# Ranking tiles laid out by chunks, with masks put together by transfers, in the sparse-attention layer of a hybrid encoder step on Trainium2

## The chip, the cores and the metric

The kernel runs on one core of one Trainium2 chip. The metric is the device time of one execution in microseconds. The engines are TensorE (PE; its weight loads are PEld), VectorE (DVE), ScalarE (ACT), GpSimd (POOL) and SyncE (SP), which here only issues DMAs. ACT and POOL issue some DMAs too.

## What is computed

One inference step of a two-layer encoder over 576 tokens: a prompt of 512 new tokens and a sample of 64 tokens that continues a stream with 512 cached ones. Layer 0 mixes by pooling, layer 1 by sparse attention; a squared-ReLU MLP follows each. The change lies in layer 1. There an indexer scores every key for every query and only the best keys take part in the attention:

```python
logits = jnp.einsum('bthd,bsd->bths', qi, kidx) * (IDX_DIM ** -0.5)         # 8 indexer heads of 64
score = jnp.einsum('bths,bth->bts', jax.nn.relu(logits), wi)                # wi: a weight per token and head
adm = (kpos[None, :] // CHUNK) <= qchunk[:, None]                           # chunks of 64 tokens
score = jnp.where(adm[None], score, NEG)
_, idx = lax.top_k(score, n_sel)                                            # n_sel = min(256, L // 4)
...
s = jnp.einsum('btgrd,btkgd->btgrk', qg, kg) * (HEAD_DIM ** -0.5)           # 16 heads of 64, 4 key heads
s = jnp.where(valid[:, :, None, None, :], s, NEG)
p = jax.nn.softmax(s, axis=-1)
o = jnp.einsum('btgrk,btkgd->btgrd', p, vg)
```

For the prompt L is 512, so 128 keys are kept of the chunks up to the query's own; a query in the first two chunks keeps all it may see. For the sample L is 576, and 144 keys are kept.

## The kernel before, in words

Activations lie feature-major (features on partitions, tokens along the row). A float32 product is made of split operands (`wh` and the rest `wl`, and the same for activations, `xs`): ACT casts `wh` (L189), DVE or POOL subtracts for `wl` (L190), and PE runs three matmuls. The weights stream from memory as `raw` tiles. Names in the trace and in the order are those of tiles.

The function `attention` projects its input with PE (`project`, tile `pj` on PSUM, 48 matmuls of 288 columns for each block of 128 features), in this order: indexer keys `ki` with the indexer weights, two blocks of indexer queries (rotated in `rope_qi`, brought to tile `qi`), keys `k`, four pairs of blocks of queries `q0` to `q3` (rotated, written to memory by DMA, read back by group as `q`), and values `V`. Then a loop over 40 units runs the attention, and at its end the output projection `wo`; blocks of it for the first tokens, `wa`, are put between units.

Tokens are taken in attention tiles i = 0 to 4: 128 prompt tokens each for i = 0 to 3, and the 64 sample tokens for i = 4. Each i has 4 groups of heads, each of two units. The units of i = 0 and 1 alternate, then come those of 2, 3 and 4. A unit's steps are: scores `sc` on PE (L1334, for the sample L1344), a softmax whose maximum DVE takes while it adds the mask (L1304, output `p` and `nm`), the exponential on ACT, the scaling of `p` on POOL (L1311, L1313), transposes `pt` on PE (L1360, L1365) and the product with the values, `o` on PE.

The mask of a tile is its ranking tile `work1` to `work4`: 128 rows by 256, 384 or 512 keys, and for the sample 64 rows by 576. `index_scores(i)` computes it head by head: two matmuls into `ix` (L1253, four for the sample, L1258), a ReLU on ACT (L1261, L1264), and a multiply-add by the token's weight on DVE (L1273, L1275). For the sample this is done on POOL (L1269, L1271). `top_k(i)` then takes rounds on DVE: MAX8 (L1286) finds the eight largest of a row, MATCH_REPLACE8 (L1287) strikes them out; 16 rounds strike 128 keys, 18 rounds 144. A last TENSOR_SCALAR (L1290) turns what was struck into 0 and the rest into a large negative number. Queries of the first two chunks of the prompt rank nothing (`mask0`).

Where the scores are written is set by `pace`, a generator that `project` steps once for each k-block: it writes one head's scores, then as many blocks later as PACE says the next. It covers all heads of the three prompt tiles but one; the rest, and the sample's eight, are written in the unit loop (`steps`). `top_k` is called ahead of the first scores of its tile's attention. The final order on each engine is made by a scheduler with a timeline simulation; an engine runs its row in that order, and SP issues its DMAs in its own.

```python
units = [Unit(i, g, s) for g in range(NKV) for i in range(2) for s in range(2)]
units += [Unit(i, g, s) for i in range(2, 5) for g in range(NKV) for s in range(2)]
```

Of the kernel before, what the change touches and what calls it, by code (L numbers as in the profile page):

```python
# [37 lines left out]
PACE = (1, 2, 2)  # L38
PACED = 3 * NIDX - 1
# [17 lines left out]
def pool_dsa_kernel(ctx: ExitStack, tc: tile.TileContext, a, o):  # L57
# [89 lines left out]
    def raw_tile(pool=raws, n=2 * 264):  # L147
        return pool.tile([P, n], F32, tag="raw", name=uid("raw"))
# [21 lines left out]
    jobs.extend(("w_v", a["w_v"][j], 4 * 264) for j in range(2))  # L170
# [6 lines left out]
    def unit(n=512):  # L177

        return [weights.tile([P, 528], F32R, tag=t, name=uid(t))[:, :n] for t in ("wh", "wl")]
# [13 lines left out]
    class Stream:  # L193
# [5 lines left out]
        def room(self, mlp):  # L199

            if "more" not in phase:
                return ("raws", raws, 2 * 264) if len(self.live["raws"]) < 2 else None
            if mlp and len(self.live["more"]) < RAWS[1]:
                return "more", phase["more"], 512
            return ("raws", raws, 2 * 264) if len(self.live["raws"]) < RAWS[0] else None

        def fill(self):
            while jobs:
# [12 lines left out]
                (nc.sync if mlp else act).dma_start(raw[-1], src[:, i * n // 2:(i + 1) * n // 2])  # L221
# [873 lines left out]
    def attention(parts):  # L1095
# [21 lines left out]
        wi = const([P, 5, 8], "wi", pool=cst)  # L1117
# [52 lines left out]
        def rope_qi(g, started=()):  # L1170

            _, st = rope(True, started)
            for part, queue in enumerate((act, nc.sync)):
                for h in range(4):
                    for j in range(2):
                        at = part * 64 + j * 32
                        queue.dma_start(f32(qi[at:at + 32, 4 * g + h]), f32(st[j][32 * h:32 * h + 32, part, P:]))
# [31 lines left out]
        turnable = tmp("wi")  # L1209
        for h, pt in enumerate(pki):  # L1210
            act.activation(halves(turnable[0:32])[:, h], pt[64:96, :HT], AF.Copy, scale=NIDX ** -0.5)
        turned_wi = psum1("wi")[:, :5 * 32].rearrange("p (i c) -> p i c", i=5)
        for i in range(5):
            n = P if i < 4 else TS
            pe.transpose(turned_wi[:n, i], turnable[0:32, i * P:i * P + n], ident[0:32, 0:32])
        for n, i in ((P, slice(0, 4)), (TS, slice(4, 5))):
            ri = r[:n, i].rearrange("p (i c) -> p i c", c=1)
            dve.tensor_tensor(wi[:n, i], turned_wi[:n, i, :NIDX], ri.to_broadcast([n, i.stop - i.start, NIDX]), ALU.mult)
        qi = const([P, NIDX, T - P], "qi", F32R, phase["queries"])
# [3 lines left out]
        project(pt, next_block(), xs)  # L1223
        t1, t2, ki = tmp("t1"), tmp("t2"), tmp("ki")
# [12 lines left out]

        rope_qi(1, [bank_halves(pt)])
        cki = split_cache(a["cache_ki"], "cki", kis)

        work = [None] + [const([P, (i + 1) * P if i < 4 else TP + TS], f"work{i}", pool=phase["under"] if i == 1 else cst) for i in range(1, 5)]

        def index_scores(i):
            np_ = P if i < 4 else TS
            wk = work[i]
            n = wk.shape[1]
            q = qi[:, :, (i - 1) * P:(i - 1) * P + np_]
            on_pool = i == 4
            for h in range(NIDX):
                if i < 4:  # L1250
                    pf = psum1("ix")
                    for part in range(2):
                        pe.matmul(pf[:, :n], q[:, h], kis[:, part, :n], start=part == 0, stop=part == 1)  # L1253
                else:
                    pf = psum("ix")
                    for part in range(2):
                        for c in range(2):
                            pe.matmul(pf[:TS, c, :HT], q[:, h], cki[:, part, c * HT:(c + 1) * HT], start=part == 0, stop=part == 1)  # L1258
                if i < 4:
                    rl = pf  # L1260
                    act.activation(rl[:, :n], pf[:, :n], AF.Relu, scale=0.125)  # L1261
                else:
                    rl = tmp("rl")
                    act.activation(halves(rl[:TS]), pf[:TS, :, :HT], AF.Relu, scale=0.125)  # L1264
                wcol = wi[:np_, i, h:h + 1]
                if on_pool:
                    dst = rl[:np_, :n] if h else wk[:np_]
                    with behind(turned):
                        pool.tensor_tensor(dst, rl[:np_, :n], wcol.to_broadcast([np_, n]), ALU.mult)  # L1269
                        if h:  # L1270
                            pool.tensor_tensor(wk[:np_], wk[:np_], dst, ALU.add)  # L1271
                elif h == 0:
                    dve.tensor_scalar(wk[:np_], rl[:np_, :n], wcol, None, ALU.mult)  # L1273
                else:
                    dve.scalar_tensor_tensor(wk[:np_], rl[:np_, :n], wcol, wk[:np_], ALU.mult, ALU.add)  # L1275
                yield
            if i < 4:
                dve.memset(wk[0:64, i * P + 64:(i + 1) * P], NEG)

        def top_k(i):  # L1280

            wk = work[i]
            np_ = P if i < 4 else TS
            for _ in range(16 if i < 4 else 18):
# [367 lines left out]
```

## Time and profile before

| | |
|---|---|
| median of 3 runs | 1074.8 us (1072.69 to 1076.98) |
| profiled execution | 1075.7 us, its span 1073.9 us, granted clock 0.996 |
| busy of the span | PE 98%, PEld 95%, DVE 85%, ACT 59%, POOL 25% |
| scoring begins on DVE | 458.32 us |
| first softmax of a unit | 535.32 us |
| output projection begins | 654.41 us |

Busy time is that in which an engine runs at least one instruction; two matmuls overlap in their ends, so the start-to-start distance is what one costs. A timeline line reads: start, duration, engine, line, operation, output tile and inputs, shape, count, and in brackets the idle time ahead and what ended it. The windows cut the span into stretches, with each engine's busy time in them. "Mean ns of one" in a group is a duration, and the last part of its line is idle time ahead of the group's instructions.

### The profile page before, as it was taken

To read this page: it belongs to the slowest core of one execution; us is meant where nothing else is said; L and a number is where in the kernel's file an instruction comes from. 1 tells how busy PE (TensorE), PEld (TensorE's weight loads), DVE (VectorE), ACT (ScalarE), POOL (GpSimd) and SP (SyncE) were. 2 spreads that over 40 slices of the span, in tenths; PEclk is the share of its full clock that TensorE was granted. 3 is DMA by queue.
4 is the path that set the end of the run, shared out by engine and by line. 5 is a ranking of instruction groups with operands and counts; after the bars stand their busy time and mean duration, and the time that the engine had idled before them with its cause. 6 is when DMAs were issued, how large, how long until landed. Compare 5 with 4: busy or idle time off the path is not lost.

```text
span 1073.9 us, 21666 instructions
## 1 busy us (share of the span) xinstructions
PE 1048.8 (98%) x7947; PEld 1024.1 (95%) x7947; DVE 908.6 (85%) x1842; ACT 630.4 (59%) x1254; POOL 269.0 (25%) x285
## 2 busy tenths in 40 slices
PE   9999999999999999999989999999999999999996
PEld 8999999999999999999989888999999999999995
DVE  7889989879978996889789974689889879979984
ACT  8556457547646764353388776556457447647742
POOL 3200111111111100358767983000111111111001
PEclk9999999999999999999999999999999999999999
DMA  8333676676676565376542444433776777676522
GB/s 250 91 104 93 166 160 166 166 169 166 148 176 169 138 182 170 111 200 168 167 131 79 134 141 140 137 101 88 177 165 150 176 167 168 148 179 162 123 59 88
DMA packets 95514, 157.68 MB, mean 147 GB/s; under 512 B 14785, under 2 KB 26352, under 8 KB 95408
## 3 DMA queue, kind: packets, MB, share of 16 engines
q1 hardware_dynamic: 67952, 108.88, 33.7%
q0 software_dynamic: 15840, 28.84, 17.4%
q10 hardware_dynamic: 11616, 18.58, 5.7%
q8 instruction: 62, 1.02, 0.4%
q14 instruction: 44, 0.36, 0.1%
HBM read 141.18 MB, written 10.89 MB: 142 GB/s over the span
## 4 chain that ended last, share of the span: by engine, by line
PE 88%; DVE 4%; DMA 3%; ACT 2%; issue 1%; POOL 1%; ACTq 0%; SPq 0%; DVEq 0%; POOLq 0%
PE b L518 32%; PE c L518 16%; PE up L316 9%; PE a L518 8%; PE pj L316 7%; PE wo L316 3%; PE wa L316 2%; PE sc L1334 2%; PE pt L1360 1%; PE pb L1062 1%; PE v L1521 1%; DMA raw<-in_w_in 1%; PE o L1392 1%; PE dn L316 1%; DVE wl L190 1%
## 5 line engine op out<-in xcount | busy, mean ns | idle before, releaser
L189 ACT CAST wh<-raw 128x512 fp32r<-128x512 f32 (+1 forms) x316 | 194.5, 619 | 210.0 <-PE b L518 64.4
L190 DVE TENSOR_TENSOR wl<-raw,wh 128x512 fp32r<-128x512 f32 x294 | 210.5, 718 | 40.9 <-ACT wh L189 34.2
L518 PE MATMUL b<-u,wh 128*128 128x288 f32 x992 | 204.1, 296 | 2.3 <-ACT a L555 1.9
L518 PEld LDWEIGHTS b<-u,wh 128*128 128x128 f32 x992 | 159.8, 188 | 4.5 <-ACT a L555 3.1
L189 ACT CAST wh<-sum 128x512 fp32r<-128x512 f32 x165 | 102.3, 620 | 96.1 <-PE b L518 42.3
L518 PE MATMUL b<-u,wl 128*128 128x288 f32 x496 | 146.1, 296 | 0.4 <-DVE wl L190 0.4
L190 DVE TENSOR_TENSOR wl<-sum,wh 128x512 fp32r<-128x512 f32 x165 | 112.3, 687 | 22.3 <-ACT wh L189 20.8
L249 POOL DMA_DIRECT2D sum<-in_w_down x31 | 27.1, 891 | 336.6 <-DVE sum L271 65.0
L518 PE MATMUL c<-u,wh 128*128 128x288 f32 x496 | 103.0, 297 | 0.0
L518 PEld LDWEIGHTS b<-u,wl 128*128 128x128 f32 x496 | 93.1, 188 | 0.6 <-DVE wl L190 0.6
L316 PE MATMUL up<-xs,wh 128*128 128x288 f32 x512 | 89.4, 296 | 0.2
L484 DVE TENSOR_TENSOR u<-v,u 128x576 fp32r<-128x576 f32 (+3 forms) x106 | 83.1, 787 | 2.1 <-ACT u L481 1.6
L518 PEld LDWEIGHTS c<-u,wh 128*128 128x128 f32 x496 | 79.8, 188 | 1.3 <-ACT wh L189 1.1
L518 PE MATMUL b<-xt,wh 128*128 128x288 f32 x384 | 77.5, 295 | 0.0
L518 PE MATMUL b<-xs,wh 128*128 128x288 f32 x384 | 77.1, 295 | 0.0
L316 PEld LDWEIGHTS up<-xs,wh 128*128 128x128 f32 x512 | 74.7, 188 | 1.0 <-DVE v L470 0.7
L481 ACT CAST u<-v 128x576 fp32r<-128x576 f32 (+3 forms) x106 | 73.7, 699 | 3.3 <-DVE v L505 2.3
L518 PE MATMUL c<-u,wl 128*128 128x288 f32 x248 | 73.2, 295 | 0.0
L249 POOL DMA_DIRECT2D sum<-in_w_up x24 | 20.7, 863 | 202.4 <-DVE wl L190 101.0
L316 PE MATMUL pj<-xs,wh 128*128 128x288 f32 x352 | 62.7, 295 | 0.0
L518 PEld LDWEIGHTS b<-xt,wh 128*128 128x128 f32 x384 | 61.7, 188 | 0.0
L518 PEld LDWEIGHTS b<-xs,wh 128*128 128x128 f32 x384 | 61.1, 188 | 0.0
(294 smaller groups left out, 2728.6 us busy)
## 6 DMA issues: line engine op xcount, KB each, us to landing
raw<-in_w_up SPq DMA_DIRECT2D x128, 256.0 KB, 3.1
raw<-in_w_down SPq DMA_DIRECT2D x128, 256.0 KB, 3.0
raw<-in_w_o ACTq DMA_DIRECT2D x32, 256.0 KB, 3.4
sum<-in_w_down SPq DMA_DIRECT2D x31, 256.0 KB, 2.9
sum<-in_w_down POOLq DMA_DIRECT2D x31, 256.0 KB, 4.9
raw<-in_w_down POOLq DMA_DIRECT2D x31, 256.0 KB, 5.0
raw<-in_w_in ACTq DMA_DIRECT2D x30, 256.0 KB, 3.1
sum<-in_w_up SPq DMA_DIRECT2D x24, 256.0 KB, 3.1
```

Of the source, the lines that this page charges most:

```text
L189: act.copy(h, src)
L190: how["sub"].tensor_tensor(l, src, f32(h), ALU.subtract)
L249: pool.dma_start(s1, odd[:, 512:], accum_op=ALU.add)
L316: pe.matmul(pt[h][:, :m] if isinstance(pt, tuple) else pt[:, h, :m], wt, xs[k][:, part, c:c + m], start=(k == 0 and i == 0), stop=(k == n ...
L481: return act.copy(u[:, f, 0], v[:, f])
L484: return dve.tensor_tensor(u[:, f, 1], v[:, f], f32(u[:, f, 0]), ALU.subtract)
L518: ins = pe.matmul(bank[:, :HT], wt, ut, start=first and j == 0 and i == 0, stop=j == 3 and i == 2, skip_group_check=True)
L1062: pe.matmul(pt[:, c0:c0 + rhs.shape[1]], lhs, rhs, start=n == 0, stop=n == len(steps) - 1)
L1334: pe.matmul(pt[:, hh, :nw], q[:, 2 * s + hh], ks[g][:, part, :nw], start=part == 0, stop=part == 1)
L1360: pe.transpose(pp[:, c:c + P], pr[:, hh, kt * P:(kt + 1) * P], ident)
L1392: pe.matmul(o[64 * hh:64 * hh + 64, s * P:(s + 1) * P], V[:, kt, vs], pT[:, c:c + P], start=kt == 0, stop=kt == i)
L1521: pe.matmul(pt[:n, :256], xs[k][:, part, i * P:i * P + n], wt[:, sl], start=(k == 0 and j == 0), stop=(k == KT - 1 and j == 2))
```

## The change

Ranking tiles are laid out by chunks. Instead of tokens 128 to 255, 256 to 383, 384 to 511 and the sample, they are now (first token, rows, keys): (128, 64, 192), (192, 128, 320), (320, 128, 448), (448, 128, 576). In a tile of two chunks the first chunk sees 64 keys less. The last tile holds the last chunk of the prompt in rows 0 to 63 and the sample in rows 64 to 127. Its index scores are made in two halves of 288 keys, each of four matmuls: the prompt's queries with zeros where the sample's would be against the prompt's keys, and zeros followed by the sample's queries against the cached ones, added up on PSUM. Its last two rounds run on the sample's rows alone.

The attention tiles stay as they were, so their masks `mask1` to `mask4` are put together: a ranking tile is written in place in the next attention tile's mask, and after its `top_k` two DMAs on SP bring the lower rows of one to the upper rows of the mask ahead (`masks[i][64:128]`), and move the upper rows of its own down (`masks[i + 1][0:64]`). What the shorter rows lack POOL fills with the negative number.

All index scores are written inside the projection, paced by (1, 2, 2, 1), and all are done ahead of V. Of the four `top_k`, two are called ahead of the first unit of i = 1, one ahead of i = 2, one ahead of i = 3. POOL ranks nothing any more. The indexer queries go to memory and come back (24 DMAs on SP for each half `g`, in place of 16 on SP and ACT from tile to tile). The indexer weights are scaled on DVE by the norm's row, not on ACT, and turned by four transposes. The value weights are loaded without the 8 columns of indexer weights, so weight tiles are 512 wide and not 528.

```diff
-PACE = (1, 2, 2)
-PACED = 3 * NIDX - 1
+PACE = (1, 2, 2, 1)
+RANKED = ((128, 64, 192), (192, P, 320), (320, P, 448), (448, P, 576))
...
+                if kind == "w_v":
+                    act.dma_start(raw[-1].rearrange("p (k c) -> p k c", k=2), src.rearrange("p (k c) -> p k c", k=4)[:, 2 * i:2 * i + 2, :256])
...
-            for part, queue in enumerate((act, nc.sync)):
-                for h in range(4):
-                    for j in range(2):
-                        at = part * 64 + j * 32
-                        queue.dma_start(f32(qi[at:at + 32, 4 * g + h]), f32(st[j][32 * h:32 * h + 32, part, P:]))
+            qd = dram.tile([2, 2, P, T - P], F32, tag=f"qi{g}", name=f"qi{g}")
+            for part in range(2):
+                for j in range(2):
+                    nc.sync.dma_start(qd[part, j], f32(st[j][:, part, P:]))
+                for j in range(2):
+                    at = part * 64 + j * 32
+                    src = qd[part, j].rearrange("(h p) t -> p h t", h=4)
+                    for to, of in ((slice(0, TP - P), slice(0, TP - P)), (slice(TP - TS, TP), slice(TP - P, T - P))):
+                        nc.sync.dma_start(f32(qi[at:at + 32, 4 * g:4 * g + 4, to]), src[:, :, of])
...
-            act.activation(halves(turnable[0:32])[:, h], pt[64:96, :HT], AF.Copy, scale=NIDX ** -0.5)
+            dve.scalar_tensor_tensor(halves(turnable[0:32])[:, h], pk[64:96, :HT], NIDX ** -0.5, halves(norm.rb[0:32])[:, h], ALU.mult, ALU.mult)
...
+                    if last:
+                        for part in range(2):
+                            for keys in (kis, cki):
+                                t0 = TP - P - TS if keys is kis else TP - P
+                                pe.matmul(pf[:, :m], qi[:, h, t0:t0 + P], keys[:, part, at:at + m],
+                                          start=part == 0 and keys is kis, stop=part == 1 and keys is cki)
...
-                if on_pool:
-                    dst = rl[:np_, :n] if h else wk[:np_]
-                    with behind(turned):
-                        pool.tensor_tensor(dst, rl[:np_, :n], wcol.to_broadcast([np_, n]), ALU.mult)
-                        if h:
-                            pool.tensor_tensor(wk[:np_], wk[:np_], dst, ALU.add)
...
-            for _ in range(16 if i < 4 else 18):
+            for n in range(18 if i == len(RANKED) - 1 else 16):
+                rows = slice(0 if n < 16 else 64, RANKED[i][1])
                 m8 = small(8, "m8")
...
+            dve.tensor_scalar(wk, wk, -2e38, NEG, ALU.is_gt, ALU.mult)
+            if i:
+                nc.sync.dma_start(masks[i][64:128], wk[0:64, :(i + 1) * P])
+                nc.sync.dma_start(masks[i + 1][0:64], masks[i + 1][64:128])
...
-                mask = work[i]
+                mask = masks[i]
...
+            due = {1: 2, 2: 1, 3: 1}
...
-                    if u + AHEAD >= 4:
-                        next(index, None)
-                    if v.i not in ranked:
-                        ranked.add(v.i)
-                        while done[0] < v.i * NIDX and next(index, 1) is None:
-                            pass
-                        top_k(v.i)
+                    for _ in range(due.pop(v.i, 0)):
+                        top_k(next(rank))
                     v.scores()
...
+        for _ in index:
+            pass
         wv = [next_block(), next_block()]
```

What this does to the order of instructions shows best on DVE, at the first softmax of attention tile i = 3 (the first ISA row that reads a 512-wide mask; in the rows here MAX, MATCH_REPLACE and TENSOR_SCALAR are ranking, ISA is a softmax). Before (`work_5889` is tile i = 3, `work_5890` the sample):

```order
L1304 ISA nm_7792 128x1
L1290 TENSOR_SCALAR work_5889<-work_5889 128x512
L1286 MAX m_1487_8366<-work_5890 64x8
L1438 TENSOR_TENSOR ot_7290<-o_7765,ot_7290 128x2x128
L1287 MATCH_REPLACE work_5890<-m_1487_8366,work_5890 64x576
L1286 MAX m_1488_8369<-work_5890 64x8
L1287 MATCH_REPLACE work_5890<-m_1488_8369,work_5890 64x576
L1304 ISA p_7904,nm_7910<-sc_7905,work_5889 128x512
L1304 ISA nm_7910 128x1
```

After (`mask_5885` is the last ranking tile, `mask_5884` the mask of i = 3):

```order
L1440 TENSOR_TENSOR ot_7508<-o_8019,ot_7508 128x2x128
L1287 MATCH_REPLACE mask_5885<-m_1400_7991,mask_5885 128x576
L1286 MAX m_1401_7994<-mask_5885 64x8
L1287 MATCH_REPLACE mask_5885<-m_1401_7994,mask_5885 64x576
L1286 MAX m_1402_7997<-mask_5885 64x8
L1287 MATCH_REPLACE mask_5885<-m_1402_7997,mask_5885 64x576
L1288 TENSOR_SCALAR mask_5885<-mask_5885 128x576
L1306 ISA p_8003,nm_8009<-sc_8004,mask_5884 128x512
L1306 ISA nm_8009 128x1
L1306 ISA p_8003,nm_8012<-sc_8004,mask_5884 128x512
```

Before, the sample's rounds stand on both sides of that softmax, fifteen of the eighteen behind it. Now all of the last tile's rounds stand ahead of it.

At the first softmax of the unit loop, on DVE too, before (ranking of the second tile ends, two splits of weights follow; in the rows after, `mask_5884` is the third ranking tile, since it is written in the place of that mask):

```order
L1286 MAX m_1276_7497<-work_5888 128x8
L1287 MATCH_REPLACE work_5888<-m_1276_7497,work_5888 128x384
L1286 MAX m_1277_7500<-work_5888 128x8
L1287 MATCH_REPLACE work_5888<-m_1277_7500,work_5888 128x384
L1290 TENSOR_SCALAR work_5888<-work_5888 128x384
L190 TENSOR_TENSOR wl_6780<-raw_6771,wh_6779 128x512
L190 TENSOR_TENSOR wl_6786<-raw_6777,wh_6785 128x512
L1304 ISA p_6937,nm_6943<-sc_6938,mask_5891 128x128
L1304 ISA nm_6943 128x1
```

After, the rows of DVE that end at the same softmax:

```order
L1286 MAX m_1287_7571<-mask_5884 128x8
L1287 MATCH_REPLACE mask_5884<-m_1287_7571,mask_5884 128x448
L1286 MAX m_1288_7574<-mask_5884 128x8
L190 TENSOR_TENSOR wl_6895<-raw_6886,wh_6894 128x512
L1287 MATCH_REPLACE mask_5884<-m_1288_7574,mask_5884 128x448
L190 TENSOR_TENSOR wl_6901<-raw_6892,wh_6900 128x512
L1286 MAX m_1289_7577<-mask_5884 128x8
L1287 MATCH_REPLACE mask_5884<-m_1289_7577,mask_5884 128x448
L1306 ISA p_7052,nm_7058<-sc_7053,mask_5881 128x128
L1306 ISA nm_7058 128x1
```

Before, two tiles were ranked by then and none begun beyond; now the first two are, and twelve rounds of the third.

On SP, at the same place as the first pair (`x` and `xd` are the residual, `in_cache_k` the cached keys, the 64-wide `q` the sample's queries). Before:

```order
L1407 DMA q_8107<-q_6758 128x4x128
L1537 DMA x_8799<-xd 128x1152
L1411 DMA q_8222<-q_6298 128x2x64 x2
L1537 DMA x_8800<-xd 128x1152
L1132 DMA raw_8227<-in_cache_k 128x512
L1411 DMA q_8343<-q_6462 128x2x64 x2
```

After, SP from the same group's queries on:

```order
L1409 DMA q_8206<-q_6873 128x4x128
L1537 DMA x_8842<-xd 128x1152
L1290 DMA mask_5884<-mask_5885 64x512
L1291 DMA mask_5885<-mask_5885 64x576
L1135 DMA raw_8326<-in_cache_k 128x512
L1413 DMA q_8321<-q_6294 128x2x64 x2
L1537 DMA x_8843<-xd 128x1152
L1413 DMA q_8442<-q_6520 128x2x64 x2
L1135 DMA raw_8447<-in_cache_k 128x512
```

The two mask transfers of the last ranking tile stand ahead of the cached keys and the sample's queries. Those of the two tiles before stand ahead of the values' output and among the queries of i = 2.

More of the change, by code (lines that the diff above doesn't have):

```diff
@@ L177, in unit @@
     def unit(n=512):
-        return [weights.tile([P, 528], F32R, tag=t, name=uid(t))[:, :n] for t in ("wh", "wl")]
+        return [weights.tile([P, 512], F32R, tag=t, name=uid(t))[:, :n] for t in ("wh", "wl")]
     def spare_unit():
@@ L1208, in attention @@
         project(pki, next_block(), xs, spread())
[L1209 to L1219, printed above, removed]
+        qi = const([P, NIDX, TP], "qi", F32R, phase["queries"])
+        pool.memset(f32(qi[:, :, TP - P:TP - TS]), 0.0)
         between = iter(())
@@ L1243, in index_scores @@
+        ranked = [masks[i + 1][:rows, :n] for i, (_, rows, n) in enumerate(RANKED)]
         def index_scores(i):
[L1244 to L1248, printed above, removed]
+            c, rows, n = RANKED[i]
+            wk = ranked[i]
+            q = qi[:, :, c - P:c - P + rows]
+            last = i == len(RANKED) - 1
             for h in range(NIDX):
-                if i < 4:
+                wcol = wi[:rows, i, h:h + 1]
+                for at in range(0, n, HT if last else n):
+                    m = min(n - at, HT) if last else n
@@ L1251, in index_scores @@
                     pf = psum1("ix")
[L1252 to L1264, printed above, removed]
@@ L1276, in index_scores @@
-                yield
-            if i < 4:
-                dve.memset(wk[0:64, i * P + 64:(i + 1) * P], NEG)
+                    if last:
[4 more added lines that the diff above has]
+                                          start=part == 0 and keys is kis, stop=part == 1 and keys is cki)
+                    else:
+                        for part in range(2):
+                            pe.matmul(pf[:rows, :m], q[:, h], kis[:, part, :m], start=part == 0, stop=part == 1)
@@ L1297, in attention @@
+        for i in range(3):
+            rows = slice(64, 128) if i else slice(0, 64)
+            pool.memset(masks[i + 1][rows, RANKED[i][2]:], NEG)
+        pool.memset(masks[0], 0.0)
+        pool.memset(masks[0][0:64, 64:128], NEG)
         both = [None] * NKV
@@ L1461, in steps @@
         def steps():
-            ranked = {0}
+            rank = iter(range(len(RANKED)))
+            due = {1: 2, 2: 1, 3: 1}
             for u in range(-AHEAD - 2, total + 2):
@@ L1491, in pace @@
             for k in range(10 * KT):
-                while due <= k and done[0] < PACED:
-                    next(index)
-                    due += PACE[min(done[0] // NIDX, 2)]
+                while due <= k:
+                    next(index, None)
+                    due += PACE[min(done[0] // NIDX, 3)]
                     done[0] += 1
@@ L1498, in attention @@
         done = [0]
-        index = (None for i in range(1, 5) for _ in index_scores(i))
-        act.activation(small(8, "e1", 1), wi[:, 0], AF.Exp)
+        index = (None for i in range(len(RANKED)) for _ in index_scores(i))
+        act.activation(small(8, "e1", 1), wi[:, 1], AF.Exp)
         between = pace()
```

52 lines of the change are left out of this document (28 added, 24 removed).

## The prediction

> **What bounds the kernel now.** I read the page first: busy shares, then the chain that ended last.
>
> ```profile
> PE 1048.8 (98%) x7947; PEld 1024.1 (95%) x7947; DVE 908.6 (85%) x1842; ACT 630.4 (59%) x1254; POOL 269.0 (25%) x285
> PE 88%; DVE 4%; DMA 3%; ACT 2%; issue 1%; POOL 1%; ACTq 0%; SPq 0%; DVEq 0%; POOLq 0%
> ```
>
> TensorE carries 88% of the chain, but these are averages, and the change touches the attention layer alone, some 220 us. So next I cut that stretch into its stages (columns: PE, PEld, DVE, ACT, POOL busy, granted clock, DMA share, GB/s).
>
> ```profile
> 458.00:465.00 7.00, 7.00 (x54) 7.00 (x54) 4.33 (x8) 4.44 (x11) 4.71 (x3) 1.00 0.66 199
> 465.00:535.00 70.00, 68.30 (x515) 67.42 (x514) 62.90 (x141) 28.47 (x53) 50.97 (x35) 1.00 0.63 178
> 535.00:592.00 57.00, 52.84 (x427) 48.72 (x425) 51.85 (x185) 47.32 (x145) 39.53 (x44) 0.97 0.37 105
> 592.00:632.00 40.00, 40.00 (x368) 34.78 (x366) 36.42 (x85) 29.65 (x62) 35.39 (x42) 1.00 0.46 133
> 632.00:655.00 23.00, 20.28 (x196) 17.03 (x195) 11.07 (x24) 17.54 (x44) 17.23 (x23) 1.00 0.49 162
> ```
>
> From 458 to 535 PE projects while DVE ranks; from 535 the attention units run. DVE is at 91% in both: it has almost the length of the stage in work, and only PE's list is longer. From 592 PE is busy all the time, and after 632 DVE is half idle. So the question is whether DVE, given other ranking work in another order, still has each mask ready when PE wants it. The timelines of DVE and PE give the marks.
>
> ```profile
> 458.32 0.48 DVE L1273 TENSOR_SCALAR work<-ix,wi 128x256 f32<-128x256 f32 x1 [3.19 <-ACT ix L1261]
> ...
> 533.30 2.04 DVE L190 TENSOR_TENSOR wl<-raw,wh 128x512 fp32r<-128x512 f32 x2 [5.79 <-ACT wh L189]
> 535.32 0.29 DVE L1304 CUSTOM_DVE_ANT_0 p<-sc,mask 128x128 f32<-128x128 f32 x1
> ...
> 592.20 0.69 DVE L1304 CUSTOM_DVE_ANT_0 p<-sc,work 128x512 f32<-128x512 f32 x1 [0.68 <-PE sc L1334]
> ...
> 631.84 0.76 DVE L1304 CUSTOM_DVE_ANT_0 p<-sc,work 128x576 f32<-128x576 f32 x1
> ```
>
> ```profile
> 654.41 0.54 PE L316 MATMUL wo<-ot,wh 128*128 128x320 f32 x2
> ```
>
> Scoring begins at 458.32; the first softmax of tokens 384 to 511 (i=3) at 592.20, waiting there for PE's scores and not for its mask; the first of the sample at 631.84; the output projection `wo` at 654.41. From `wo` on nothing changes, so the forecast is the shift of that 654.41.
>
> **The change, part by part.**
>
> *Top-k.* A round is a MAX8, a value load and a MATCH_REPLACE8:
>
> ```profile
> L1286 DVE MAX8 m<-work 64x8 f32<-64x576 f32 x18 | 13.5, 749 | 0.3
> L1286 DVE MAX8 m<-work 128x8 f32<-128x512 f32 x16 | 11.0, 688 | 0.1
> L1286 DVE MAX8 m<-work 128x8 f32<-128x384 f32 x16 | 8.9, 555 | 0.2
> L1286 DVE MAX8 m<-work 128x8 f32<-128x256 f32 x16 | 6.8, 423 | 0.3
> L1287 DVE MATCH_REPLACE8 work<-m,work 64x576 f32<-64x576 f32 x18 | 13.2, 734 | 0.0
> ...
> L1287 DVE MATCH_REPLACE8 work<-m,work 128x512 f32<-128x512 f32 x16 | 10.8, 674 | 0.0
> ```
>
> ```profile
> 623.77 0.75 DVE L1286 MAX8 m<-work 64x8 f32<-64x576 f32 x1
> ...
> 625.40 0.75 DVE L1286 MAX8 m<-work 64x8 f32<-64x576 f32 x1
> ```
>
> The time follows the columns, not the rows (64x576 lies on the line of the 128-row ones), and a round of 576 takes 1.63 us from start to start. That is twice its MAX8 plus 0.13; so 512 takes 1.51, 384 1.24, 256 0.98. MAX8 falls by 1.02 ns a column from 576 to 256, which gives 448 1.37, 320 1.11, 192 0.85. Over the whole stage: before 16 x (0.98 + 1.24 + 1.51) + 18 x 1.63 = 89.0; after 16 x (0.85 + 1.11 + 1.37) + 18 x 1.63 = 82.6. The merged tile saves 6.4 us of DVE in sum. But what counts is what stands ahead of 592.20. In the order before, three of the sample's rounds stand there and fifteen behind: 59.7 + 4.9 = 64.6. In the order after, all four top-ks do, since the last one now also makes the mask of i=3: 82.6. So +18.0 at the mark, though −6.4 in sum.
>
> *Scoring on DVE.*
>
> ```profile
> L1275 DVE SCALAR_TENSOR_TENSOR work<-ix,wi,work 128x512 f32<-128x512 f32 x7 | 5.1, 733 | 0.0
> L1275 DVE SCALAR_TENSOR_TENSOR work<-ix,wi,work 128x384 f32<-128x384 f32 x7 | 4.3, 609 | 0.0
> L1275 DVE SCALAR_TENSOR_TENSOR work<-ix,wi,work 128x256 f32<-128x256 f32 x7 | 3.4, 483 | 1.9 <-ACT ix L1261 1.5
> ```
>
> Before: 8 x (0.483 + 0.609 + 0.733) = 14.6. After, by the same line: 8 x (0.42 + 0.546 + 0.67) + 16 x 0.515 (288 wide) = 21.3. The sample's scoring comes from POOL to DVE: +6.7, all ahead of the mark. Sum at the mark +24.7. Between other instructions a round loses less (a round of 576 is 0.749 + 0.734 + about 0.08 of instructions, 0.07 of its 1.63 is waiting for itself), and more rounds now stand so; counted row by row in the two orders the surplus is 21. I take 21, ends 18 and 25.
>
> *What of it is hidden.* DVE's idle time from 458 to 592 is 2.67 + 7.10 + 5.15 = 14.9 by the stages above. The 5.79 at 533.30 will be filled, since rounds of the third tile stand ahead of the first softmax now. I leave half idle: the first scores still wait for queries, softmaxes for PE. So 21 − 7.5 = 13.5 late.
>
> *The mask transfers.* Ahead of the first i=3 softmax now stands a transfer of 64x512 that SP issues only after the last rank instruction. The nearest rows:
>
> ```profile
> raw<-in_w_up SPq DMA_DIRECT2D x128, 256.0 KB, 3.1
> ...
> qi<-st SPq DMA_DIRECT2D x16, 56.0 KB, 2.0
> ```
>
> 128 KB I put at 2.3; between the two, nearer the smaller; ends 2.0 and 3.1. [...] The second transfer (64x576) is for the sample alone and has 25 us. The two pairs for earlier tiles have slack: tile 2 is ranked some 12 rounds ahead of its first use, tile 3 about 48 DVE rows ahead. On SP, what is queued behind the last pair (cache keys, the sample's queries, `x`) is issued near 608 in both kernels. First i=3 softmax: 592.2 + 13.5 + 2.3 = 608, bounds 603 and 613.
>
> *From there to `wo`.* Before, 654.41 − 592.20 = 62.2, of it PE busy about 59.7 (40.00 + 20.28 less the matmuls behind 654.41). Two blocks of `wa`, two pairs of i=3 scores and the end of i=2 will lie ahead of the mark now, since PE, waiting for DVE, has run everything else. A block is 24 matmuls at a pitch of (588.51 − 588.16) / 3 = 0.118 us, 2.84:
>
> ```profile
> 588.16 0.40 PE L316 MATMUL wa<-ot,wh 128*128 128x256 f32 x2
> ...
> 588.51 0.40 PE L316 MATMUL wa<-ot,wh 128*128 128x256 f32 x2
> ```
>
> 2 x 2.84 + 2 x 0.95 + about 3 = 10.6 less. Against it the first softmax, exponential, POOL scaling and transposes now stand bare: softmaxes of 0.69 and three other engines, some 4 us, of which I count 2 beyond the present gaps. 62.2 − 10.6 + 2 = 53.6, bounds 48.5 and 57. `wo` at 608 + 53.6 = 661.6: +7.
>
> *TensorE.* Index matmuls by pitch, two of 512 columns 0.46, four of the sample 0.6 (0.61 below):
>
> ```profile
> 477.26 0.63 PE L1253 MATMUL ix<-kis,qi 128*128 128x512 f32 x2
> 477.72 0.42 PE L316 MATMUL pj<-xs,wl 128*128 128x288 f32 x2
> ...
> 551.66 0.77 PE L1258 MATMUL ix<-cki,qi 128*64 128x288 f32 x4
> 552.27 0.64 PE L1334 MATMUL sc<-k,q 128*128 128x256 f32 x4
> ```
>
> In proportion the three tiles of before cost 8 x (0.23 + 0.345 + 0.46) = 8.3 and the sample 4.8, together 13.1. After, 64 matmuls of 288 at 0.133 (the pitch of `wa`'s 256, by columns) to 0.15 are 8.5 to 9.6, the three narrower tiles 8 x (0.17 + 0.29 + 0.40) = 6.9; 15 to 18, the upper end if the narrowest don't scale. So +2 to +5, and all of it in the projection now: the units' first scores come some 4 us later on PE. DVE's lateness covers that; without it, it would cost 3.
>
> *Waits that may go.*
>
> ```profile
> PE sc L1334 <- DMA q<-q: 2.4, 1, 2.4
> PE ix L1253 <- DVE work L1275: 1.7, 1, 1.7
> PE wi L1215 <- ACT wi L1211: 1.2, 1, 1.2
> ```
>
> The `wi` wait goes (−1.2 on PE, ahead of scoring), for DVE now makes it a block later. The one for `q` may move: the fourth group's queries still leave SP behind V's output. Both lie before the mark and change it only through DVE's start.
>
> *POOL, ACT, DMA.*
>
> ```profile
> L1271 POOL TENSOR_TENSOR work<-work,rl 64x576 f32<-64x576 f32 x7 | 9.9, 1414 | 0.3
> L1269 POOL TENSOR_TENSOR rl<-rl,wi 64x576 f32<-64x576 f32 x7 | 8.0, 1142 | 5.1 <-ACT rl L1264 5.1
> 454.60 3.27 ACTq L1177 DMA_DIRECT2D qi<-st x5
> ```
>
> POOL loses 19 us in the units; it stands before the softmax chain only in 1.4 us pieces, and I credit −1. The queries by DRAM are two transfers in a row (2.0 each) where one was, but no longer eight issues in a row on ACT of 0.65 each (3.27 for five); the scores start within 1 us of now, either way. The value weights' narrower strided loads and the POOL memsets lie beside PE work of many us: nothing, and if a load were late PE's `v` would show it.
>
> Sum: +7 − 1 = +6 on the profiled 1075.7, which is 0.9 above the median of the runs shown: 1081.5.
>
> **Rivals.**
>
> (1) *Faster.* DVE does not bind at the mark: 16 of its 21 us surplus vanish in idle time and easier contention. For it: 14.9 idle, and splits that cost 1078 ns in this stretch against 718 over the whole kernel:
>
> ```profile
> L190 DVE TENSOR_TENSOR wl<-raw,wh 128x512 fp32r<-128x512 f32 x21 | 22.4, 1078 | 11.6 <-ACT wh L189 11.5
> ```
>
> That is up to 21 x 0.36 = 7.6. Then the waits above (5.3) and the 2.7 gap behind 632 go, since the sample's mask is no longer last, less 2 for the index matmuls: −6, 1069.7. It decides if the first i=3 softmax comes before 597. Against it: the splits share SBUF with POOL's rotations, which stay.
>
> (2) *No change.* The mark is late, but the tail of i=3 and the sample, with 24 us of rounds less beside them, runs tighter: 48.5 + 606 = 654.5, ±2.5. For it: after 592 DVE was at 91%; against: PE was at 40.00 of 40 there.
>
> (3) *Slower by more.* Waits compound: PE stands for several us before the first i=3 transposes, and the clock falls. 2.4 us of waiting before 546.49 left this:
>
> ```profile
> 546.00:550.00 4.00, 3.51 (x17) 3.54 (x18) 1.71 (x6) 1.73 (x6) 1.40 (x1) 0.57 0.06 15
> ```
>
> That is 0.57 for four us, 1.7 us lost. Seven rounds, 11.4 us, and the transfer stand between the last i=2 softmax and the first i=3 one; with the mark at 613 and 57 behind it `wo` is at 670: about +14, 1090. The Trainium skill ("TensorE: Matmul & The Clock Gate", What's actually happening) has the clock halved after an idle window of about 3.4 us and as long to come back: 1.7 us more each time. The row shows the fall after a shorter wait.
>
> **How the numbers follow.** The forecast (+2 to +10) has 0.50, (1) 0.12, (2) 0.22, (3) 0.16. A measurement of this kernel can tell about 0.5%, 5.4 us, from nothing. Over half of the forecast's case lies above that: slower 0.27 + 0.16, rounded 0.45; same 0.23 + 0.22 and a little of (1), 0.45; faster 0.10. The range leaves out half of (1) and little of (3): 1070.5 to 1090.5.
>
> **What would show it.** Right: first i=3 softmax at 603 to 613, waiting for the mask's transfer; DVE nearly without idle from 460 to there; PE with 10 us or more of idle between 540 and 608, charged to DVE; 48 to 57 us from there to `wo`; no POOL ranking; `v` without waits. Wrong: a first i=3 softmax before 598, or one that waits for PE's scores as now.

## The result, and the profile after

The changed kernel takes 1085.69 us (median of 4 runs, 1084.36 to 1086.59) against 1074.51 us before (4 runs in all): ratio 1.0102, 95% interval 1.0079 to 1.0125. It is 11 us slower. The span of its profiled execution is 1084.0, 10.1 above that of the profiled execution before. Of all executions in this document one, of `after_qi_direct`, fell out of line: it took 2626.77 us, the other four of that kernel 1095.05 to 1099.14, and its ratio is made without it.

The page of the changed kernel, its busy shares and its chain:

```profile
PE 1052.3 (97%) x7978; PEld 1027.8 (95%) x7978; DVE 902.1 (83%) x1859; ACT 630.8 (58%) x1260; POOL 247.5 (23%) x274
PE 84%; DVE 6%; DMA 4%; ACT 2%; POOL 1%; issue 1%; SPq 0%; ACTq 0%; DVEq 0%; POOLq 0%
```

DVE has 6.5 us less work in the whole span and POOL 21.5 less; yet DVE's share of the chain rose from 4 to 6%, and DMA's from 3 to 4%. (By groups of instructions the rounds on DVE, value loads included, fell from 84.9 to 78.3 us, and the scores that came over from POOL took the same 6.6 back, 14.6 to 21.2; what is left of the 6.5 is mostly splits that got cheaper, 330.3 to 324.6.) DVE and POOL do less, PE only 3.5 us more, and the kernel is 11 us slower: when the work is done must count for much of it.

The marks in the changed kernel, from the timelines of DVE and PE:

```profile
460.39 0.40 DVE L1273 TENSOR_SCALAR mask<-ix,wi 64x192 f32<-64x192 f32 x1
...
548.71 0.28 DVE L1306 CUSTOM_DVE_ANT_0 p<-sc,mask 128x128 f32<-128x128 f32 x1
...
609.44 0.69 DVE L1306 CUSTOM_DVE_ANT_0 p<-sc,mask 128x512 f32<-128x512 f32 x1 [2.34 <-DMA mask<-mask]
...
636.84 0.76 DVE L1306 CUSTOM_DVE_ANT_0 p<-sc,mask 128x576 f32<-128x576 f32 x1 [2.87 <-PE sc L1346]
```

```profile
545.57 1.52 PE L1336 MATMUL sc<-k,q 128*128 128x256 f32 x12
...
663.73 0.54 PE L319 MATMUL wo<-ot,wh 128*128 128x320 f32 x2
```

The first softmax of i=3 comes at 609.44 (before 592.20) and waits 2.34 us for the mask's transfer; `wo` begins at 663.73 (before 654.41), 9.3 later, and the other 0.8 of the 10.1 lies behind it, where PE has a new wait of 0.75 us at 694.47, for DVE's `x`. The units begin on PE at 545.57; before it was 534.67:

```profile
534.67 1.52 PE L1334 MATMUL sc<-k,q 128*128 128x256 f32 x12
```

So the units start 10.9 later and take 1.6 less. That looks as if the whole loss were made in the projection.

That start varies in the kernel before itself, though. `before_v_act` and `before_sample_first` below leave its projection as it is, and PE runs the same order there; their profiles have the units' start at 537.71 and 538.02. PE's wait for DVE's scoring near 470 is 2.98 and 2.99 us in them and 1.70 in the profile before, and what stands behind it differs too. First a window of the kernel before, then one of `before_v_act`:

```profile
470.00:474.00 4.00, 4.00 (x29) 4.00 (x29) 3.90 (x10) 2.65 (x7) 2.29 (x3) 1.00 0.77 255
```

```profile
471.00:475.00 4.00, 3.73 (x15) 3.73 (x16) 3.79 (x11) 2.67 (x6) 1.45 (x2) 0.60 0.68 218
```

The granted clock stays at 1.00 in the one and is 0.60 in the other. Some 3 of the 10.9 us therefore belong to this one profile of the kernel before, and not to the change.

What PE waits for in the projection and in the units, from the waits of the changed kernel:

```profile
PE ix L1269 <- DMA qi<-qi: 4.6, 1, 4.6
PE pt L1362 <- POOL p L1315: 3.7, 2, 3.3
PE pt L1362 <- ACT p L1307: 2.5, 1, 2.5
PE o L1400 <- ACT pT L1373: 1.3, 2, 0.7
PE pj L319 <- DVE rp L1153: 1.1, 1, 1.1
```

The largest wait is new: the second half of the indexer queries comes 4.6 us late by way of DRAM. The waits for `wi` (1.2) and for DVE's scoring (1.7) are gone, and so is the 2.4 for `q`. The second line, 3.3 of it at 613.61, is the lateness of i=3 as PE sees it: PE waits for POOL, which waits for ACT and the softmax at 609.44.

Two causes fit these lines. Either the units' late start is what counts (a longer projection), or DVE's ranking ahead of the i=3 mask would have been late anyway, and the late start is hidden behind it. In the expectations below, theory P is the longer projection, theory Q the late queries in it, and theory T DVE's ranking ahead of the i=3 mask. The stretch from the first scores to that softmax, before and after:

```profile
458.00:592.20 134.20, 128.35 (x993) 123.34 (x993) 119.08 (x333) 80.23 (x208) 95.41 (x80) 0.99 0.52 148
```

```profile
458.00:609.44 151.44, 142.80 (x1124) 136.94 (x1122) 135.28 (x394) 82.01 (x220) 81.07 (x72) 0.98 0.51 146
```

DVE is busy 119.08 of 134.20 before and 135.28 of 151.44 after: 16.2 more, idle 16.2 instead of 15.1. The page alone can't say which of the two binds. The experiments do.

### The profile page after: what moved, and what is told of

Read it like the earlier page. It is cut to its first block, busy times and chain, and to the rows that moved or that the text cites. A ratio compares the mean times of both kernels' runs of the same rounds, so it can differ in the third digit from the quotient of the medians.

```text
span 1084.0 us, 21740 instructions
## 1 busy us (share of the span) xinstructions
PE 1052.3 (97%) x7978; PEld 1027.8 (95%) x7978; DVE 902.1 (83%) x1859; ACT 630.8 (58%) x1260; POOL 247.5 (23%) x274
## 4 chain that ended last, share of the span: by engine, by line
PE 84%; DVE 6%; DMA 4%; ACT 2%; POOL 1%; issue 1%; SPq 0%; ACTq 0%; DVEq 0%; POOLq 0%
PE b L521 32%; PE c L521 16%; PE up L319 9%; PE a L521 8%; PE pj L319 6%; PE wa L319 2%; PE pb L1065 1%; DVE mask L1287 1%; PE pt L1362 1%; PE dn L319 1%; PE sc L1336 1%; PE o L1394 1%; DVE wl L190 1%; DVE m L1286 1%; DMA qi<-st 1%
## 5 line engine op out<-in xcount | busy, mean ns | idle before, releaser
L189 ACT CAST wh<-raw 128x512 fp32r<-128x512 f32 x316 | 194.6, 620 | 207.8 <-PE b L521 62.9
L190 DVE TENSOR_TENSOR wl<-raw,wh 128x512 fp32r<-128x512 f32 x294 | 205.7, 701 | 36.1 <-ACT wh L189 29.5
```

Of the source, the lines that this page charges most:

```text
L189: act.copy(h, src)
L190: how["sub"].tensor_tensor(l, src, f32(h), ALU.subtract)
```

## The experiments

Each was timed beside the kernel before on its own chip; ratios are to that, and the changed kernel's is 1.0102.

**Less DVE work ahead of the mark.**

```diff
-            for n in range(18 if i == len(RANKED) - 1 else 16):
-                rows = slice(0 if n < 16 else 64, RANKED[i][1])
+            for n in range(9 if i == len(RANKED) - 1 else 16):
+                rows = slice(0, RANKED[i][1])
```

> The changed kernel with 9 rounds in place of 18 on the last ranking tile (leaves out half of that tile's selection, so its masks keep fewer keys): 9 x 1.63 = 14.7 us less DVE work, all ahead of the first i=3 softmax. Theory T: that softmax comes 10 to 14 us earlier, and the time falls by 5 to 9 us, down to where TensorE alone sets it. Theories Q and P: the units begin as late as now, TensorE is the bound from there, and the time falls by 2 us or less.

Measured: 1079.68 us, ratio 1.0025 (1.0014 to 1.0035): by the ratios three quarters of the loss are gone, by the profiled spans (1077.8 against 1084.0) 6.2 of 10.1 us. In its timeline:

```profile
546.82 1.52 PE L1336 MATMUL sc<-k,q 128*128 128x256 f32 x12
...
658.39 0.55 PE L319 MATMUL wo<-ot,wh 128*128 128x320 f32 x2
```

```profile
598.35 0.69 DVE L1306 CUSTOM_DVE_ANT_0 p<-sc,mask 128x512 f32<-128x512 f32 x1 [3.19 <-PE sc L1336]
```

The units begin even later than in the changed kernel (546.82), and still `wo` is 5.3 earlier: the softmax comes 11.1 earlier and waits for PE's scores now. A late start alone did not cost the time; PE runs the units in 111.6 us when DVE lets it, 118.2 in the changed kernel.

**Less PE work in the projection.**

```diff
-                        for part in range(2):
+                        for part in range(1):
                             for keys in (kis, cki):
```

> The changed kernel with half of the index matmuls of the last ranking tile (leaves out the low part of the split keys there: 32 matmuls of 288 columns, 32 x 0.133 = 4.3 us of TensorE in the projection). Theory P: 3 to 4.5 us faster. Theory T: the units begin 4 us earlier, but DVE has the same work ahead of the first i=3 softmax, which moves by less than 1.5 us, and so does the time. Theory Q: the wait for the queries lies ahead of these matmuls and stays at 4 to 5 us.

Measured: 1086.74 us, ratio 1.0095 (1.0079 to 1.0111): nothing gained. The units begin at 541.44, 4.1 earlier, as reckoned, and then:

```profile
612.37 0.69 DVE L1306 CUSTOM_DVE_ANT_0 p<-sc,mask 128x512 f32<-128x512 f32 x1 [4.21 <-DMA mask<-mask]
```

```profile
616.25 0.48 PE L1362 MATMUL pt<-ident,p 128*128 128x128 f32 x1 [9.50 <-POOL p L1315]
```

The i=3 softmax is not earlier (612.37), and PE's wait behind it grew from 3.30 to 9.50. What PE won in the projection it stood still for in front of i=3. That is as theory T has it, and against P. (I had expected that softmax within 1.5 us; it came 2.9 later. 1.9 of it is the transfer, 4.21 in place of 2.34, and 1.0 DVE's ranking, which ended later; why was not followed up.)

**The same mechanism made in the kernel before, with no work added.**

```diff
+                        if v.i == 3:
+                            while next(index, 1) is None:
+                                pass
+                            top_k(4)
+                        if v.i < 4:
-                        top_k(v.i)
+                            top_k(v.i)
```

> The kernel before with one change: the sample's top-k is called ahead of that of tile i=3, not behind it. No matmul, no transfer and no byte is added; the fifteen of its rounds that stood behind the first i=3 softmax stand ahead of it, 15 x 1.63 = 24.5 us, with its two cuts of 1.9. Theory T: that softmax comes 14 to 22 us later than 592.2 (DVE's idle time of some 8 us takes up a part) and, with 48 to 57 us from there to wo, the kernel is 6 to 16 us slower. Rival P (the loss of the changed kernel is its longer projection): no difference over 2 us, since DVE's sum of work and the units' start stay as they were.

Measured: 1109.09 us, ratio 1.0312 (1.0291 to 1.0333): 33 us slower, twice the top of what I expected. From its timelines:

```profile
636.30 0.69 DVE L1304 CUSTOM_DVE_ANT_0 p<-sc,work 128x512 f32<-128x512 f32 x1
```

```profile
PE pt L1360 <- POOL p L1313: 33.1, 1, 33.1
```

The units began at 538.02 and the i=3 softmax at 636.30, 44 later, with one wait of PE of 33.1 us. I had counted 24.5 + 1.9 and some idle time taken up; instead DVE's busy time from 458 to the mark grew by 29.2 (119.08 to 148.30) and its idle time by 14.9 (15.1 to 30.0). The rounds that had filled the gaps of the first units were those of i=3, and these now queue behind a tile whose scores come late: POOL ends the sample's last score at 569.67, and the first of its rounds begins at 570.10. It shows how much the order alone is worth: this kernel has the instructions of the one before.

**The way of the queries.** First by DRAM alone, in the kernel before:

```diff
-                        queue.dma_start(f32(qi[at:at + 32, 4 * g + h]), f32(st[j][32 * h:32 * h + 32, part, P:]))
+                    nc.sync.dma_start(qd[part, j], f32(st[j][:, part, P:]))
...
+                    nc.sync.dma_start(f32(qi[at:at + 32, 4 * g:4 * g + 4]), src)
```

> The kernel before with the one part that brings the indexer queries by way of DRAM on SP (four writes and four reads for each half). Theory Q: 3 to 6 us slower than the kernel before, with a wait of TensorE's index matmuls for a query transfer of 3 us or more. Theory P and theory T: no difference over 1 us, since no matmul and no ranking is added.

Measured: 1079.12 us, ratio 1.0022 (1.0010 to 1.0034). Slower by 2.4 us, less than the 3 I set for theory Q and more than the 1 I allowed the others, though PE waits 2.87 and 0.70 for `qi`, and its units begin 3.8 later than in the profile before (0.8 and 0.5 later than in the two other profiles named above). `wo` begins 1.3 later.

Then the old way in the changed kernel:

```diff
+                        for to, of in ((slice(0, TP - P), slice(P, TP)), (slice(TP - TS, TP), slice(TP, T))):
+                            queue.dma_start(f32(qi[at:at + 32, 4 * g + h, to]), f32(st[j][32 * h:32 * h + 32, part, of]))
```

> The changed kernel with the indexer queries brought from tile to tile as before (two transfers for each of 16 pieces, since the sample's columns now stand apart; half on ACT, half on SP), not by way of DRAM. Theory Q (the second half of the queries comes 4.56 us too late for the index matmuls, and TensorE's clock is low for some us behind that wait; the loss is carried to the end): 4 to 6 us faster than the changed kernel, near 1080, and no wait of TensorE for a query transfer over 1 us. Theory P (16 us of index matmuls in the projection, 8 more than before, is what delays the units): at most 1 us faster. Theory T (the forecast: DVE's ranking ahead of the first i=3 softmax sets it): that softmax stays within 2 us of 609.4 and the time within 2 us.

Measured: 1096.74 us, ratio 1.0185 (1.0169 to 1.0202): all three were wrong on this one, for it is no clean undoing. The sample's columns stand apart, so there are 64 issues and not 32, half of them on ACT, ahead of the ReLUs. From ACT's and DVE's timelines:

```profile
460.89 8.46 ACTq L1181 DMA_DIRECT2D qi<-st  x13
469.40 0.95 ACT L1267 ACTIVATE ix<-ix 64x192 f32<-64x192 f32 x4 [8.53 <-DMA qi<-st]
```

```profile
469.73 0.41 DVE L1270 TENSOR_SCALAR mask<-ix,wi 64x192 f32<-64x192 f32 x1 [8.38 <-ACT ix L1267]
...
621.79 0.69 DVE L1303 CUSTOM_DVE_ANT_0 p<-sc,mask 128x512 f32<-128x512 f32 x1 [2.52 <-POOL ck L306]
```

DVE's first scores come at 469.73, 9.3 later than 460.39, and the i=3 softmax 12.4 later than 609.44. PE has no wait for a query left, and the units begin at 548.97, only 3.4 later. The time follows DVE.

Last, the way by DRAM on two queues:

```diff
-            for part in range(2):
+            for part, queue in enumerate((act, nc.sync)):
                 for j in range(2):
-                    nc.sync.dma_start(qd[part, j], f32(st[j][:, part, P:]))
+                    queue.dma_start(qd[part, j], f32(st[j][:, part, P:]))
...
-                        nc.sync.dma_start(f32(qi[at:at + 32, 4 * g:4 * g + 4, to]), src[:, :, of])
+                        queue.dma_start(f32(qi[at:at + 32, 4 * g:4 * g + 4, to]), src[:, :, of])
```

> The changed kernel with the indexer queries' way by DRAM dealt to two queues, the high parts on ACT, the low parts on SP: 6 issues in a row for each half in place of 12. Theory Q and theory T agree here: the wait of 4.56 us for the second half falls to 2 us or less, DVE scores 4 to 5 us earlier, and the time falls by 3 to 5 us. Rival R (the issues hold ACT up, as 32 of them did in after_qi_direct, and the first scores come later on DVE): no gain, or a loss up to 5 us.

Measured: 1084.65 us, ratio 1.0070 (1.0049 to 1.0090); beside 1.0102 (1.0079 to 1.0125) this is 3 us at best, and the intervals overlap. The wait of 4.56 fell to 0.55, with 2.43 at the first half instead, so that 1.6 of it went in sum. The units begin 1.7 earlier, but:

```profile
609.74 0.69 DVE L1306 CUSTOM_DVE_ANT_0 p<-sc,mask 128x512 f32<-128x512 f32 x1 [3.68 <-DMA mask<-mask]
```

The i=3 softmax did not move (609.44), nor did `wo` (663.74 against 663.73): DVE ended its ranking 1.0 earlier, and the mask's transfer took 1.3 longer. So what was won in the projection was not won at the mark; what the whole 4.56 us are worth this run does not show, as most of the wait only moved.

**Two rounds taken from ahead of the mark, and all together.**

```diff
+            rounds(16, slice(0, RANKED[i][1]))
+            cut(slice(0, 64) if last else slice(0, RANKED[i][1]))
             if i:
                 nc.sync.dma_start(masks[i][64:128], wk[0:64, :(i + 1) * P])
+                if last:
+                    rounds(2, slice(64, 128))
+                    cut(slice(64, 128))
```

> The changed kernel, with the last ranking tile cut in two behind its 16th round: rows 0 to 63 are turned into the mask and moved at once, and the two rounds of the sample's rows alone, with their cut, come behind. Theory T (DVE's work ahead of the first i=3 softmax, and the transfer, set the time): 2 x 1.63 = 3.3 us less ahead of that softmax, part of it fills the 2.3 us of the transfer, so the softmax comes 3 to 4 us earlier and the time falls by 2 to 4 us. Rival (what is late is the start of the units, 10.9 us behind the kernel before): no change over 1 us.

Measured: 1087.07 us, ratio 1.0090 (1.0071 to 1.0109): no gain that can be told. From the units' start to the i=3 softmax it took 60.7 us in place of 63.9, which is the 3.2 expected; but the units began 2.2 later, so the softmax came 1.0 earlier (608.40) and not 3 to 4. The greater part of the two rounds ran while the mask's transfer was under way; the last MATCH_REPLACE8 and its cut, 1.2 us, stood behind the first four i=3 softmaxes. From the first of these to `wo` it took 58.2, not 54.3, and why was not tested apart.

```diff
-        wv = [next_block(), next_block()]
+        wv = [next_block(pool), next_block(pool)]
```

> The changed kernel with both of these edits, and the splits that are made while V is projected (the first weights of wa) given to POOL, which ranks no more, and not to DVE: four splits of 0.7 to 1.1 us less on DVE ahead of the first softmax. Theory T: the first i=3 softmax 10 to 14 us earlier than 609.4, the time 6 to 10 us less than the changed kernel's, which is the kernel before within 4 us. Rival P: the index matmuls keep the units' start 5 us or more behind the kernel before, and the time stays 5 us or more above it.

(The two edits are those of `after_qi_two` and `after_late_rounds`.) Measured: 1085.11 us, ratio 1.0070 (1.0047 to 1.0094). The profiled execution has the i=3 softmax at 601.93, 7.5 earlier, less than the 10 to 14 of theory T, and `wo` at 660.32. Its runs spread from 1081.99 to 1089.30, and the gain of 6 to 10 us was not there.

> The kernel after_three with half of the index matmuls of the last tile (leaves out the low part of the split keys there; 4.3 us of TensorE in the projection). In the changed kernel the same cut gained nothing. If DVE is no longer late in after_three, and TensorE's list from the units' start on is the bound (rival P as the second limit), the units begin 4 us earlier and the time falls by 3 to 4.5 us. If DVE still binds there (theory T alone), it falls by less than 1.5 us.

This is the edit of `after_ix_half` on top. Measured: 1083.86 us, ratio 1.0069 (1.0053 to 1.0084), the same as without. The units begin 3.1 earlier, the softmax comes at 603.76 and not earlier than 601.93, and PE waits 3.90 us in front of i=3. So in that kernel too DVE is late, and a second limit by PE is not seen.

**A version that beats both.** Here the edits take away waits that the kernel before lists for PE.

```diff
-        nc.sync.dma_start(o["v_p"], V[:, 0:4])
-        nc.sync.dma_start(o["v_s"], V[:TS, 8])
+        act.dma_start(o["v_p"], V[:, 0:4])
+        act.dma_start(o["v_s"], V[:TS, 8])
```

> The kernel before with the two DMAs of the values' output issued by ACT and not by SP, where the last group's queries stood queued behind them until V was done. It tells what the 2.40 us wait of TensorE for q was worth there: with the low clock behind it (0.57 for four us) 2 to 4 us faster if the wait goes; no difference if TensorE then waits for DVE at the same place.

Measured: 1073.36 us, ratio 0.9971 (0.9957 to 0.9984): 3 us faster. The wait for `q` is 0.46.

```diff
-            act.activation(halves(turnable[0:32])[:, h], pt[64:96, :HT], AF.Copy, scale=NIDX ** -0.5)
+            dve.scalar_tensor_tensor(halves(turnable[0:32])[:, h], pk[64:96, :HT], NIDX ** -0.5, halves(norm.rb[0:32])[:, h], ALU.mult, ALU.mult)
```

> A version meant to beat both: before_v_act with the indexer weights made as the change makes them (scaled on DVE by the norm's row, turned a block of projection later). TensorE's wait of 1.23 us for wi at 433.8 goes; 0 to 1.5 us faster than before_v_act, so 2 to 5 us faster than the kernel before. Rival: the two DVE instructions (0.8 us) and the copies delay the keys' rotation and the first scores, and nothing is gained.

Measured: 1067.45 us, ratio 0.9918 (0.9903 to 0.9933): 8 to 9 us faster than the kernel before, more than the 2 to 5 I had set, and 20 faster than the changed one. Two windows of it, the projection and the units:

```profile
465.00:531.00 66.00, 66.00 (x499) 65.40 (x498) 61.94 (x143) 28.96 (x56) 49.06 (x33) 1.00 0.66 188
...
535.00:592.00 57.00, 54.51 (x463) 50.11 (x463) 55.20 (x188) 49.10 (x147) 40.54 (x47) 1.00 0.36 102
```

PE is busy in every microsecond from 465 to the units, which begin at 531.54. More went than the 1.23 for `wi`: the wait for DVE's scoring at 470 went with it (1.70 in the kernel before, 2.98 in `before_v_act`), and the clock stays at 1.00. Against `before_v_act` the units begin 6.2 earlier, and these account for it: 1.2, 3.0, and some 1.6 for the low clock behind the second wait (0.40 of 4 us). Why that second wait went was not tested apart.

> The same with the first tile's index matmuls spread by two k-blocks each and not by one (PACE 2, 2, 2), so that the wait of 1.7 to 3.0 us of TensorE's index matmuls for DVE's scoring at 470 goes. 1 to 3 us faster than before_v_act_wi if that wait was on the path; no difference, or slower, if the later scores delay DVE's ranking, as theory T has it.

```diff
-PACE = (1, 2, 2)
+PACE = (2, 2, 2)
```

Measured: 1068.19 us, ratio 0.9923 (0.9908 to 0.9938): no difference, there being no wait left to take.

## Why the prediction was right, and where its steps were off

The time, 1085.69, lies in the range of 1070.5 to 1090.5, and the sign was the forecast's; 11 us came where the sum carried 6. The sum's last line does not follow from it: 6 on 1075.7 is 1081.7, and less the 0.9 it is 1080.8, where 1081.5 was written. Nothing else hangs on that.

*The mechanism and its two marks held.* The i=3 softmax was put at 608 and came at 609.44; it waits for the mask's transfer, put at 2.3, measured 2.34. From there to `wo` 53.6 were reckoned and 54.3 measured. `after_last_9`, `after_ix_half` and `before_sample_first` show that DVE's order ahead of that mask is the cause and not only a coincidence of numbers.

*DVE's surplus was too large, its idle time too small, and the place of the mark is in part luck.* I took 21 us more of DVE work at the mark and let 7.5 of 14.9 us idle take up a part. Measured: 16.2 more, and of the idle time 1.3 taken up (16.2 idle, with the 2.34 of the transfer in it, where it was 15.1). So the sign "DVE nearly without idle from 460 to there" was wrong. Work was put 4.8 too high and the filling 6.2 too high; the two cancelled but for 1.4, and that is why 609.44 stands so near 608. The rounds and scores were near the interpolated prices:

```profile
L1286 DVE MAX8 m<-mask 128x8 f32<-128x448 f32 x16 | 10.0, 623 | 0.3
L1286 DVE MAX8 m<-mask 128x8 f32<-128x320 f32 x16 | 7.8, 485 | 0.1
...
L1275 DVE SCALAR_TENSOR_TENSOR mask<-ix,wi,mask 64x192 f32<-64x192 f32 x7 | 2.9, 409 | 7.9 <-ACT ix L1270 7.4
L1286 DVE MAX8 m<-mask 64x8 f32<-64x192 f32 x16 | 5.5, 346 | 0.1
```

623, 485 and 346 ns against 619, 488 and 358. What was left out is the splits. From 458 to the mark of each kernel, first before, then after:

```profile
L190 DVE TENSOR_TENSOR wl<-raw,wh 128x512 fp32r<-128x512 f32 x14 | 15.4, 1112 | 5.8 <-ACT wh L189 5.8
L190 DVE TENSOR_TENSOR wl<-raw,wh 128x528 fp32r<-128x528 f32 x4 | 3.7, 934 | 0.0
L190 DVE TENSOR_TENSOR w<-raw,w 128x512 fp32r<-128x512 f32 x1 | 1.4, 1358 | 0.5 <-ACT w L189 0.5
```

```profile
L190 DVE TENSOR_TENSOR wl<-raw,wh 128x512 fp32r<-128x512 f32 x17 | 16.0, 947 | 1.4 <-ACT wh L189 1.4
```

19 splits took 20.5 us, and 17 take 16.0: 4.5 less, two fewer and each shorter. I had named cheaper splits for the faster rival and credited 1 for POOL. POOL is less busy in the projection (38.31 us of 70 from 465 to 535, where it was 50.97). In both traces from 420 to 680, each `wl` split of a `raw` tile that is listed singly and has nothing on POOL beside it took 0.67 to 0.70 us, and each of 0.74 or more, up to 1.91, had a POOL instruction beside it; some beside POOL took no longer. So the long ones go with POOL's work, though no run took that work away by itself. The idle in front of the 192-wide scores, 6.99 us of it ending at 470.25 behind PE's wait for the second half of the queries, is what was not filled.

*"The scores start within 1 us of now, either way"* is the step that failed: the queries by DRAM were put at nothing. Twelve DMAs stand in a row on one queue for each half, reads behind writes (24 in all, and not for each half, as the part on the change has it). The first scores came 2.1 later (460.39 against 458.32), and PE waited 4.56 us for the second half, which left DVE idle where I had counted on its filling up. In the kernel before, alone, the detour cost 2.4 us.

*TensorE's term was netted against the wrong place.* 15 to 18 us of index matmuls were reckoned and the pitches give about 16; but the sample's 4.8 had stood in the units, so the projection grew by 8 and with the late queries the units began 10.9 later, some 3 of which are the variation shown above, and not 4. "DVE's lateness covers that" was right for the 4.1 us that `after_ix_half` took away: it gained nothing. It also made one of my signs wrong: I looked for 10 us of PE idle between 540 and 608, but PE had its late start instead, and only 4.1 idle up to the mark.

*The −1 for POOL and the rest behind `wo`* make the other part of the gap: 9.3 at `wo` where I carried 7 and took 1 off for POOL, and 0.8 behind it, the wait of 0.75 for `x`, which I put at nothing.

*Rivals.* (1) needed the mark ahead of 597: it wasn't. (2) needed 48.5 us from the mark to `wo`: 54.3. Of (3), the clock fell as its row said. Two windows of the changed kernel, behind the wait for the queries and in front of i=3, and one of `after_ix_half`:

```profile
469.50:473.00 3.50, 3.48 (x19) 3.50 (x20) 1.99 (x5) 1.03 (x4) 0.48 (x1) 0.57 0.44 168
```

```profile
613.60:617.00 3.40, 3.39 (x12) 2.77 (x12) 1.04 (x3) 2.73 (x8) 3.40 (x5) 0.53 0.19 40
```

```profile
616.00:619.50 3.50, 3.25 (x12) 2.76 (x13) 1.02 (x5) 1.60 (x6) 3.40 (x6) 0.50 0.00 0
```

The granted clock is 0.50 to 0.57 for some 3.5 us behind waits of 4.56, 3.30 and 9.50, about 1.5 to 1.75 us lost each time. The Trainium skill ("TensorE: Matmul & The Clock Gate", What's actually happening) has half clock after an idle window of about 3.4 us and full clock after as long a busy one. The recovery agrees: behind the wait of 3.30 the clock is 0.53 up to 617.00 and 1.00 from 617.00 to 620.50. The fall came after 3.30 here and after 2.40 in the kernel before, so a wait need not be as long as the window; and it did not come after every such wait, for behind 2.48 in `after_last_9` (550.80 to 554.30) and 3.15 in `after_qi_direct` (500.40 to 504.00) the clock is 1.00. It is a part of the mechanism here, not a case of its own.

What stays open: `after_last_9` is still 0.25% above the kernel before. Its units begin 12 us later than in the profile before and 9 later than in the two other profiles of the same projection, and how the late queries, the added index matmuls and the six mask transfers share that rest was not separated.

## What to carry to other kernels

When work is merged, count it at each point where somebody waits for a part of it, not in sum: here the merged tile saved DVE 6.6 us of rounds and made the mask of i=3 wait for rounds that had run behind it. Where two engines are both near full, a cut on one is worth what the other leaves: test the binding one by taking work away ahead of its deadline, as removing 4 us of matmuls, or 1.6 us of waiting for queries, gained nothing that can be told here while removing 15 us of ranking gained 6 to 8. A wait in a stage where PE has no slack counts together with the clock behind it: the 2.40 us in the kernel before and the 2.98 in `before_v_act` left 0.57 and 0.60 for four us, while the 1.23 and 1.70 in the kernel before left 1.00. One profile of a kernel is one draw: with the same order on PE the units' start lay 3 us apart.

## What the runs showed of the hardware that was not expected

Reordering without adding an instruction cost 33 us (`before_sample_first`), with a PE clock of 0.50 in the 3.5 us behind the wait of 33.1. A DMA issue on ACT's own queue took 0.65 us, and 13 in a row (8.46 us) kept its ReLUs waiting 8.5 us. Reading back from DRAM in 192 KB pieces took 4.0 us from issue to landing where one transfer of 56 KB from tile to tile took 2.0:

```profile
qi<-st SPq DMA_DIRECT2D x8, 224.0 KB, 3.4
qi<-qi SPq DMA_DIRECT2D x8, 192.0 KB, 4.0
```

A write of 3.4 and a read of 4.0 in a row are the price of the detour; I had reckoned 2.0 each.
